# Which filter taps run on VectorE, and where the rest of them is added up

## The chip, the cores and the metric

The kernel runs on one core of a Trainium2 chip. TensorE (PE in the profile) multiplies matrices, VectorE (DVE), ScalarE (ACT) and GpSimd (POOL) work on elements, and SyncE (SP) issues the loads. The metric is the device time of one execution in microseconds (us). Three runs of the kernel before took 558.88, 558.89 and 561.23 us; the median is 558.89.

## The reference, cut to what matters

One decoder layer on 256 positions of width 1024. The input is normed and projected; two mixers run side by side, a convolution module and a sparse attention with three branches; their gated sum, a cross-attention and a feed-forward net follow. The change touches the first mixers only:

```python
def conv_module(u, dw_w, dw_b, ln_g, ln_b, pw_w):
    a, gt = jnp.split(u, 2, axis=-1)
    v = a * jax.nn.sigmoid(gt)
    v = lax.conv_general_dilated(v, dw_w[:, None, :], window_strides=(1,),
        padding=((CONV_WIDTH - 1, 0),), feature_group_count=CONV_CH, ...) + dw_b   # 31 taps per channel
    v = jax.nn.silu(layer_norm(v, ln_g, ln_b))
    return v @ pw_w
...
p_cmp = masked_softmax(s_c, dist_c >= 0)                       # compressed branch: 15 blocks of keys
o_cmp = jnp.einsum("bgrsn,bngd->bsgrd", p_cmp, v_cmp)
...
p = masked_softmax(s, mask)                                    # selected and window branch, head by head
```

## The kernel before, in words

Channels lie on the 128 partitions and positions along the free axis, so the 1024 channels of the convolution are eight blocks of 128 channels by 256 positions (with 30 columns of padding ahead). A tap multiplies one shifted block by one weight per channel and adds it to the block's sum.

**Weights.** Each weight matrix comes in halves of 128 x 1024 numbers. `split` (L173, L175) makes two parts of a half for three reduced matmuls (`rows`, L240): ScalarE copies the high part, and the difference, the low part, is made by GpSimd for the matrices from u1 to ga1 and by VectorE for all others. A load buffer (four of them) is free again when both parts are made; the parts have five buffers each. A low part is used by TensorE in the third of its three rounds.

**Taps.** `tapped` runs the taps of two blocks in turn on VectorE: the first tap is a `tensor_scalar` (L406), each other one a `scalar_tensor_tensor` (L408) that reads the shifted block from SBUF and the running sum from PSUM; the last one writes to `yt`. All four pairs of blocks go through one generator, and `convolve(n, ...)` draws n tap instructions from it at given places in the program: 13 behind each projection u1 to u7, 14 behind kc and vc, 11 behind each q, and so on, and what is left behind vw. They get a late priority there, so the scheduler lays them into gaps of VectorE's order. The last pair (blocks 6 and 7) stops eight taps early; `late_taps` makes those eight: ScalarE multiplies (L420, one instruction for each block), GpSimd adds to `yt` (L421, one for both blocks), and this needs VectorE's part of `yt` to be complete.

**Start of the attention heads.** The gates ga and gc, the compressed scores and the scores of the heads follow on TensorE. VectorE adds the bias to the compressed scores (L664), takes the minimum and subtracts it (L804, L805); ScalarE takes the exponential (L810); VectorE sums, inverts and multiplies (L811 to L816). For each pair of heads `scores` reduces (L707, L712), ScalarE exponentiates (L722, L726), and `weights` makes the row sum (L729), its reciprocal (L731) and eight multiplications (L734, L736) on VectorE. TensorE then transposes the compressed weights (L848) and the heads' weights (L747). VectorE also makes the masked values `vcm` (L829), which TensorE needs in `output`. The layer norm of the convolution begins with `layer_norm_sum` on GpSimd (L599, L601, L293); its mean is used on TensorE in the turn of the third pair of heads.

The order on each engine is set by the tile scheduler from the program's order, priorities and the marks of `behind(...)` ("issue only after these"). Each engine works strictly through its own order.

## Time and profile before

The profiled execution took 558.54 us; its span on the core is 556.7 us.

| what | us |
|---|---|
| TensorE busy | 543.3 (98% of the span) |
| VectorE busy | 467.1 (84%) |
| ScalarE busy | 349.5 (63%) |
| GpSimd busy | 129.9 (23%) |
| mean granted clock of TensorE | 0.994 |
| VectorE busy from 100 to 180 us | 78.5 of 80 |
| GpSimd busy from 40 to 140 us | 83.3 of 100 |

A row of the timeline has start and length in us, engine, line, operation, output and inputs, shape and count; what stands in brackets is the idle time of the engine just before and what ended it. A row of the waits has who waited for whom, the total in us, how often and the longest. A row of windows has the busy time of each engine in a stretch, then TensorE's granted clock (1.00 is full), the share of the DMA engines and GB/s.

### The profile page before, as it was taken

Reading aid. Unit: us, or ns where it says so; the run is one execution under the profiler, and the core shown is the slowest. Engines: PE = TensorE matmul, PEld = TensorE weight load, DVE = VectorE, ACT = ScalarE, POOL = GpSimd, SP = SyncE. Lnnn points to the kernel's source line nnn. Section 1 sums busy time; section 2 is a strip of 40 time slices with the busy share of each in tenths; the row PEclk is TensorE's granted clock in tenths of the full one; section 3 lists DMA queues with packets and bytes.
Section 4 is the critical chain, followed back from the end, with each engine's and each line's share of the span. In section 5 each row is a group of like instructions: output and inputs, shape, how many; then the busy total and the mean of one; then the engine's idle time right before and its main releaser. Section 6 shows DMA issues by size and latency. Waiting matters only on the chain.

```text
span 556.7 us, 10484 instructions
## 1 busy us (share of the span) xinstructions
PE 543.3 (98%) x3976; PEld 502.8 (90%) x3976; DVE 467.1 (84%) x940; ACT 349.5 (63%) x622; POOL 129.9 (23%) x86
## 2 busy tenths in 40 slices
PE   9999999999997899999999999999999999999995
PEld 7999999999997798998999999988888888888774
DVE  3987898999999988795768676577899998869996
ACT  4763466666464887779646655466666676655563
POOL 0089798788009200300003100150000000000000
PEclk9999999999999999999999999999999999999998
DMA  8938936465251654335555733545645654525541
GB/s 303 399 113 276 351 107 225 159 203 186 77 167 42 194 167 132 97 113 173 180 191 172 270 119 100 172 144 162 216 152 194 203 198 162 176 89 190 195 146 75
DMA packets 29155, 97.32 MB, mean 175 GB/s; under 512 B 3120, under 2 KB 5680, under 8 KB 28848
## 3 DMA queue, kind: packets, MB, share of 16 engines
q1 hardware_dynamic: 28384, 95.42, 51.4%
q10 hardware_dynamic: 720, 1.23, 0.6%
q8 instruction: 31, 0.51, 0.4%
q14 instruction: 20, 0.16, 0.1%
HBM read 95.39 MB, written 1.25 MB: 174 GB/s over the span
## 4 chain that ended last, share of the span: by engine, by line
PE 82%; DVE 11%; DMA 3%; ACT 2%; issue 1%; ACTq 0%; DVEq 0%; SPq 0%
PE ps_f L1131 15%; PE ps_u L240 8%; PE ps_f L1133 7%; PE ps_pw L240 4%; PE ps_q L240 4%; PE ps_xq L240 4%; PE ps_v L240 4%; PE ps_wo L240 4%; PE ps_xo L240 4%; PE ps_k L240 3%; PE ps_ga L240 3%; PE ps_gc L240 2%; DMA fo<-in_wfo_dram 2%; DVE fo_1l L175 2%; DVE tr L1074 2%
## 5 line engine op out<-in xcount | busy, mean ns | idle before, releaser
L408 DVE SCALAR_TENSOR_TENSOR yp<-vt,ppt,yp 128x256 f32<-128x256 f32 x216 | 86.8, 481 | 0.3
L1131 PE MATMUL ps_f<-g,f_1h 128*128 128x512 f32 x176 | 48.9, 397 | 0.0
L1131 PE MATMUL ps_f<-g,f_0h 128*128 128x512 f32 x176 | 48.3, 396 | 0.0
L1131 PEld LDWEIGHTS ps_f<-g,f_1h 128*128 128x128 f32 x176 | 32.8, 188 | 7.5
L1131 PEld LDWEIGHTS ps_f<-g,f_0h 128*128 128x128 f32 x176 | 30.1, 188 | 4.0
L175 DVE TENSOR_TENSOR f_1l<-f,f_1h 128x1024 fp32r<-128x1024 f32 x22 | 27.5, 1248 | 5.5 <-ACT f_1h L173 4.0
L1133 PEld LDWEIGHTS ps_f<-g,f_0l 128*128 128x128 f32 x176 | 27.0, 189 | 3.9
L175 DVE TENSOR_TENSOR f_0l<-f,f_0h 128x1024 fp32r<-128x1024 f32 x22 | 26.8, 1218 | 1.7 <-ACT f_0h L173 1.7
L1133 PE MATMUL ps_f<-g,f_0l 128*128 128x256 f32 x176 | 28.2, 282 | 0.0
L173 ACT ACTIVATE f_1h<-f 128x1024 fp32r<-128x1024 f32 x22 | 23.2, 1057 | 7.4 <-PE ps_xo L240 3.7
L1133 PE MATMUL ps_f<-g,f_1l 128*128 128x256 f32 x176 | 26.5, 281 | 0.0
L175 POOL TENSOR_TENSOR u_0l<-u,u_0h 128x1024 fp32r<-128x1024 f32 x7 | 17.4, 2491 | 31.4 <-DVE kt L486 29.8
L173 ACT ACTIVATE f_0h<-f 128x1024 fp32r<-128x1024 f32 x22 | 23.1, 1050 | 1.4 <-PE ps_xo L240 1.3
L1134 ACT ACTIVATE ab<-ps_f 128x256 f32<-128x256 f32 x44 | 16.6, 377 | 10.9 <-PE ps_f L1133 10.2
L1133 PEld LDWEIGHTS ps_f<-g,f_1l 128*128 128x128 f32 x176 | 23.3, 188 | 0.0
L1135 DVE TENSOR_TENSOR ab<-ps_f,ab 128x256 f32<-128x256 f32 x44 | 18.4, 419 | 5.3 <-ACT ab L1134 5.0
L722 ACT ACTIVATE p<-p,mins 128x256 f32<-128x256 f32 x32 | 15.9, 499 | 10.3 <-DVE mins L707 10.3
L284 ACT ACTIVATE uh<-sl 128x256 fp32r<-128x256 f32 x22 | 9.1, 414 | 14.6 <-DVE sl L1139 14.6
L421 POOL TENSOR_TENSOR yt<-yt,vw 128x512 f32<-128x512 f32 x8 | 11.6, 1455 | 28.3 <-DVE yt L408 27.8
L175 POOL TENSOR_TENSOR u_1l<-u,u_1h 128x1024 fp32r<-128x1024 f32 x7 | 18.0, 2578 | 0.0
L1138 ACT ACTIVATE sl<-ab 128x256 f32<-128x256 f32 x22 | 9.2, 417 | 13.5 <-DVE ab L1136 13.5
L173 ACT ACTIVATE fo_1h<-fo 128x1024 fp32r<-128x1024 f32 x10 | 10.6, 1057 | 8.8 <-DMA fo<-in_wfo_dram 7.1
(613 smaller groups left out, 1669.9 us busy)
## 6 DMA issues: line engine op xcount, KB each, us to landing
f<-in_wst_dram SPq DMA_DIRECT2D x44, 512.0 KB, 6.0
fo<-in_wfo_dram SPq DMA_DIRECT2D x22, 512.0 KB, 4.2
u<-in_wst_dram SPq DMA_DIRECT2D x14, 512.0 KB, 7.6
q<-in_wst_dram SPq DMA_DIRECT2D x8, 512.0 KB, 5.2
ga<-in_wst_dram SPq DMA_DIRECT2D x8, 512.0 KB, 3.4
gc<-in_wst_dram SPq DMA_DIRECT2D x8, 512.0 KB, 3.8
v<-in_wst_dram SPq DMA_DIRECT2D x8, 512.0 KB, 5.7
pw<-in_wst_dram SPq DMA_DIRECT2D x8, 512.0 KB, 4.6
```

Of the source, the lines that this page charges most:

```text
L173: copy = nc.scalar.activation(hi, w, AF.Copy)
L175: splits[name] = copy, eng.tensor_tensor(out=lo, in0=w, in1=f(hi[:]), op=ALU.subtract)
L240: mm = nc.tensor.matmul(ps[:, b], lhsT=lhsT, rhs=rhs, start=row + b + kb == 0, stop=kb == NB - 1 and row == 2 and b == 1)
L408: nc.vector.scalar_tensor_tensor(out=yt[:, k] if t == ts[-1] else acc[i], in0=v, scalar=w, in1=acc[i], op0=ALU.mult, op1=ALU.add)
L421: nc.gpsimd.tensor_tensor(out=yt[:, j:j + 2], in0=yt[:, j:j + 2], in1=pr, op=ALU.add)
L722: exp.append(nc.scalar.activation(p1[k][:, br], p1[k][:, br], AF.Exp, scale=-1.0, bias=mins[:, hd, 1, br:br + 1], accum_out=sums[:, hd, 1, ...
L1074: return nc.vector.tensor_tensor(out=tr[:, to], in0=pick(a), in1=pick(b), op=ALU.subtract)
L1131: nc.tensor.matmul(ps, lhsT=hs[kb // 4][0][:, kb % 4, cs], rhs=fg[:, :, kb], start=kb == 0, stop=False)
L1133: nc.tensor.matmul(ps[:, 1], lhsT=hs[kb // 4][1][:, kb % 4, cs], rhs=fg[:, 0, kb], start=False, stop=kb == NB - 1)
L1134: nc.scalar.activation(ab[:, b], ps[:, 0], AF.Copy)
L1135: nc.vector.tensor_tensor(out=ab[:, b], in0=ps[:, 1], in1=ab[:, b], op=ALU.add)
L1138: silu = nc.scalar.activation(sl, ab[:, 0], AF.Silu)
```

## The change

Of the first pair of blocks, taps 0 to 17 go to ScalarE and GpSimd, and taps 18 to 30 stay on VectorE and end in a separate tile `part01`. ScalarE writes tap 0 with the bias straight into `yt`, each other tap into a buffer (four of them, tag "vw"); GpSimd adds the seventeen buffers and at last `part01`. The other three pairs have all 31 taps on VectorE, and `late_taps` is gone. `convolve` takes two numbers now: how many tap instructions of VectorE to draw (as before) and how many taps of the other generator. The masked values are made by GpSimd behind the low part of the second half of ga0, and `layer_norm_sum` stands behind the last multiplication of the compressed softmax.

```diff
-LATE = 8
+FIRST_G = 18
...
-    def tapped(j, ts):
+    def taps_v(j, ts, out):
         acc = [aux(f"yp{j + i}", [P, S], "pt", 2) for i in range(2)]
...
-                if t == 0:
-                    nc.vector.tensor_scalar(out=acc[i], in0=v, scalar1=w, scalar2=col(PP_DB, k), op0=ALU.mult, op1=ALU.add)
+                if t == ts[0]:
+                    nc.vector.tensor_scalar(out=acc[i], in0=v, scalar1=w, scalar2=col(PP_DB, k) if t == 0 else 0.0,
+                                            op0=ALU.mult, op1=ALU.add)
...
-    taps = chain(*[tapped(j, range(TAPS - LATE * (j == 6))) for j in range(0, NB, 2)])
-
-    def late_taps(j, *marks):
-
-        with behind(*marks):
-            for t in range(TAPS - LATE, TAPS):
-                pr = small(f"vw{j}_{t}", [P, 2, S], tag="vw", bufs=4)
-                for i in range(2):
-                    nc.scalar.activation(pr[:, i], vt[j + i][:, t:t + S], AF.Copy, scale=col(PP_DW + TAPS * (j + i), t))
-                nc.gpsimd.tensor_tensor(out=yt[:, j:j + 2], in0=yt[:, j:j + 2], in1=pr, op=ALU.add)
+    def taps_g(ts):
+
+        for t in ts:
+            pr = yt[:, 0:2] if t == 0 else small(f"vw{t}", [P, 2, S], tag="vw", bufs=4)
+            for i in range(2):
+                nc.scalar.activation(pr[:, i], vt[i][:, t:t + S], AF.Identity, scale=col(PP_DW + TAPS * i, t),
+                                     bias=col(PP_DB, i) if t == 0 else 0.0)
+            if t > 0:
+                nc.gpsimd.tensor_tensor(out=yt[:, 0:2], in0=yt[:, 0:2], in1=pr, op=ALU.add)
+            yield
+        nc.gpsimd.tensor_tensor(out=yt[:, 0:2], in0=yt[:, 0:2], in1=part01, op=ALU.add)
+        yield
+
+    part01 = small("part01", [P, 2, S], tag="pr", bufs=4)
+    taps = range(TAPS)
+    on_v = chain(taps_v(0, taps[FIRST_G:], part01), *[taps_v(j, taps, yt[:, j:j + 2]) for j in range(2, NB, 2)])
+    on_g = taps_g(taps[:FIRST_G])
...
-        convolve(13 * (j > 0), act, vec)
+        convolve(13 * (j > 0), (0, 1, 1, 1, 1, 0, 1, 1)[j], act, vec)
...
-        convolve(13 + NB * TAPS * br, act, splits[name + "_1"][0])
+        convolve(13 + NB * TAPS * br, 1 + TAPS * br, act, splits[name + "_1"][0])
...
+    hm = cpt[:, CP_HM:CP_HM + 8].unsqueeze(2).to_broadcast([P, 8, HD])
+    with behind(splits["ga0_1"][1]):
+        for i in range(2):
+            nc.gpsimd.tensor_tensor(out=vcm[:, 8 * i:8 * i + 8], in0=vcs[:, i].unsqueeze(1).to_broadcast([P, 8, HD]), in1=hm, op=ALU.mult)
...
-    late_taps(6, splits["ga1_1"][1])
...
-    total = layer_norm_sum()
+    with behind(vec):
+        total = layer_norm_sum()
...
-                with behind(*first["scores"]):
-                    hm = cpt[:, CP_HM:CP_HM + 8].unsqueeze(2).to_broadcast([P, 8, HD])
-                    for i in range(2):
-                        nc.vector.tensor_tensor(out=vcm[:, 8 * i:8 * i + 8], in0=vcs[:, i].unsqueeze(1).to_broadcast([P, 8, HD]),
-                                                in1=hm, op=ALU.mult)
```

In the changed file the lines move: a tap on VectorE is L409, one on ScalarE L418, an add L421, the add of `part01` L423, the mask L660, the norm's sum L608 and L610; the heads' weights are L742 (sum), L744 (reciprocal), L747 and L749 (multiplications), their score reductions L720 and L725, the exponentials L735 and L739, the compressed softmax L817, L818, L823 and L824 to L829, its transposes L857. TensorE's order is the same in both. Three places of the other engines' orders follow (names end in a running number of the tile).

GpSimd from the last weight splits (`ga_0l`, `ga_1l`) to the sum of the norm, before and then now:

```order
L175 TENSOR_TENSOR ga_0l<-ga_0_1924,ga_0h 128x1024
L175 TENSOR_TENSOR ga_1l<-ga_1_1967,ga_1h 128x1024
L421 TENSOR_TENSOR yt<-yt,vw_23_2013 128x512
L421 TENSOR_TENSOR yt<-yt,vw_24_2017 128x512
...
L421 TENSOR_TENSOR yt<-yt,vw_28_2033 128x512
L599 TENSOR_TENSOR ysum<-yt 128x512
L421 TENSOR_TENSOR yt<-yt,vw_29_2037 128x512
L421 TENSOR_TENSOR yt<-yt,vw_30_2041 128x512
L601 TENSOR_TENSOR ysum<-ysum,yt 128x512 x2
```

```order
L175 TENSOR_TENSOR ga_0l<-ga_0_1978,ga_0h 128x1024
L421 TENSOR_TENSOR yt<-yt,vw_1763 128x512
L660 TENSOR_TENSOR vals<-vcs,cpt 128x512 x2
L175 TENSOR_TENSOR ga_1l<-ga_1_2021,ga_1h 128x1024
L421 TENSOR_TENSOR yt<-yt,vw_1867 128x512
...
L421 TENSOR_TENSOR yt<-yt,vw_1887 128x512
L423 TENSOR_TENSOR yt<-yt,part_362 128x512
L608 TENSOR_TENSOR ysum<-yt 128x512
L610 TENSOR_TENSOR ysum<-ysum,yt 128x512 x2
```

Eleven of the seventeen adds now stand between earlier splits (the last of these is the second row here), and six behind the last split; before, all eight stood there.

VectorE at the compressed scores (`nsc`), before and then now:

```order
L664 TENSOR_TENSOR nsc<-cs_ps_1995,nsc 128x256
L175 TENSOR_TENSOR ga_1l<-ga_1_2217,ga_1h 128x1024
L175 TENSOR_TENSOR gc_0l<-gc_0_2277,gc_0h 128x1024
L175 TENSOR_TENSOR gc_1l<-gc_1_2307,gc_1h 128x1024
L408 SCALAR_TENSOR_TENSOR yp_1718<-vt_354,ppt,yp_1718 128x256
L408 SCALAR_TENSOR_TENSOR yt<-vt_354,ppt,yp_1717 128x256
L804 TENSOR_REDUCE mc<-nsc 128x32
L408 SCALAR_TENSOR_TENSOR yt<-vt_354,ppt,yp_1718 128x256
L805 TENSOR_TENSOR nsc<-nsc,mc 128x512
L729 SCALAR_TENSOR_TENSOR sums<-sums,igd 128x8
```

```order
L678 TENSOR_TENSOR nsc<-cs_ps_2049,nsc 128x256 x2
L175 TENSOR_TENSOR ga_1l<-ga_1_2239,ga_1h 128x1024
L175 TENSOR_TENSOR gc_0l<-gc_0_2297,gc_0h 128x1024
L817 TENSOR_REDUCE mc<-nsc 128x32
L175 TENSOR_TENSOR gc_1l<-gc_1_2327,gc_1h 128x1024
L818 TENSOR_TENSOR nsc<-nsc,mc 128x512
L742 SCALAR_TENSOR_TENSOR sums<-sums,igd 128x8
```

The last taps (`yp`, `yt`) are gone from this place; they stand ahead of the first `nsc` add now.

VectorE between the scores of the second and third pair of heads (`p_4` and `p_5` are third-pair score tiles, `p_2` and `p_3` second-pair ones), before and then now:

```order
L829 TENSOR_TENSOR vals<-vcs,cpt 128x512 x2
L175 TENSOR_TENSOR gc_0l<-gc_0_2384,gc_0h 128x1024
...
L769 SCALAR_TENSOR_TENSOR sga<-sga,o_2398 128x256
L707 ISA p_4_2419,mins<-s_4_2414,nb_2409 128x256
...
L712 ISA p_2_2413,mins<-s_2_2412,nb_2409 128x128
L712 ISA mins 128x1
L729 SCALAR_TENSOR_TENSOR sums<-sums,igd 128x8
L175 TENSOR_TENSOR gc_0l<-gc_0_2676,gc_0h 128x1024
L731 RECIPROCAL sums<-sums 128x8
L734 TENSOR_SCALAR p_2_2259<-p_2_2259,sums 128x256
```

```order
L782 SCALAR_TENSOR_TENSOR sga<-sga,o_2418 128x256
L720 ISA p_4_2439,mins<-s_4_2434,nb_2429 128x256
L720 ISA mins 128x1
L742 SCALAR_TENSOR_TENSOR sums<-sums,igd 128x8
L720 ISA p_4_2439,mins<-s_4_2434,nb_2429 128x256
L720 ISA mins 128x1
L744 RECIPROCAL sums<-sums 128x8
L720 ISA p_5_2447,mins<-s_5_2442,nb_2429 128x256
...
L747 TENSOR_SCALAR p_2_2281<-p_2_2281,sums 128x256
```

The mask (`vals`) and one weight split no longer stand ahead of the second pair's multiplications, and the row sum and reciprocal stand inside the third pair's reductions.

More of the change, by code (lines that the diff above doesn't have):

```diff
@@ L404, in tapped, with convolve @@
                 v, w = vt[k][:, t:t + S], col(PP_DW + TAPS * k, t)
-                if t == 0:
-                    nc.vector.tensor_scalar(out=acc[i], in0=v, scalar1=w, scalar2=col(PP_DB, k), op0=ALU.mult, op1=ALU.add)
+                if t == ts[0]:
+                    nc.vector.tensor_scalar(out=acc[i], in0=v, scalar1=w, scalar2=col(PP_DB, k) if t == 0 else 0.0,
+                                            op0=ALU.mult, op1=ALU.add)
                 else:
-                    nc.vector.scalar_tensor_tensor(out=yt[:, k] if t == ts[-1] else acc[i], in0=v, scalar=w, in1=acc[i],
+                    nc.vector.scalar_tensor_tensor(out=out[:, i] if t == ts[-1] else acc[i], in0=v, scalar=w, in1=acc[i],
                                                    op0=ALU.mult, op1=ALU.add)
                 yield
-    taps = chain(*[tapped(j, range(TAPS - LATE * (j == 6))) for j in range(0, NB, 2)])
-    def late_taps(j, *marks):
-        with behind(*marks):
-            for t in range(TAPS - LATE, TAPS):
-                pr = small(f"vw{j}_{t}", [P, 2, S], tag="vw", bufs=4)
-                for i in range(2):
-                    nc.scalar.activation(pr[:, i], vt[j + i][:, t:t + S], AF.Copy, scale=col(PP_DW + TAPS * (j + i), t))
-                nc.gpsimd.tensor_tensor(out=yt[:, j:j + 2], in0=yt[:, j:j + 2], in1=pr, op=ALU.add)
-    def convolve(n, *marks):
+    def taps_g(ts):
[13 more added lines that the diff above has]
+    on_g = taps_g(taps[:FIRST_G])
+    def convolve(n_v, n_g, *marks):
         here = tc.cur_priority
@@ L427, in convolve @@
         with behind(*marks):
-            for _ in range(n):
-                next(taps, None)
+            for work, n in ((on_v, n_v), (on_g, n_g)):
+                for _ in range(n):
+                    next(work, None)
         tc.cur_priority = here
@@ L488, in tile_hybrid_block @@
                                     ppt[:, PP_POS + 16 * kv:PP_POS + 16 * kv + 16].rearrange("p (m l) -> p l m", m=2))
-        convolve(14, act, vec)
+        convolve(14, 1 - kv, act, vec)
     kcp = small("kcp", [P, GROUPS, 2, 16], F32R)
@@ L544, in tile_hybrid_block @@
                                              op0=ALU.mult, op1=ALU.subtract)
-        convolve(11, act, vec)
+        convolve(11, (1, 0, 1, 1)[j], act, vec)
         if j == 1:
@@ L559, in keys @@
                                           in1=f(kdh[lo:lo + 64, g::2, br]), op=ALU.subtract)
-        convolve(11, act, vec)
+        convolve(11, 1 - br, act, vec)
     keys(0, gemm("ks", h))
```

## The prediction

> **What bounds the kernel now.** I read the page's busy shares first, then the waits of TensorE (PE), then the order of time around the two waits that are large, and from there the engines that ended them.
>
> ```profile
> PE 543.3 (98%) x3976; PEld 502.8 (90%) x3976; DVE 467.1 (84%) x940; ACT 349.5 (63%) x622; POOL 129.9 (23%) x86
> PE pc_ps L848 <- DVE nsc L816: 3.7, 1, 3.7
> PE pt_a L747 <- DVE p L736: 1.6, 1, 1.6
> ```
>
> PE is busy for 98% of the span, so the change can only win where PE waits or runs slow. Both large waits lie in the stage that starts the attention heads, and VectorE (DVE) ends both. TensorE there, start and length in us, with the same transposes in an undisturbed place (215 us) below; the last row is the window behind the first wait (busy us of PE, weight load, DVE, ACT and POOL, then granted clock, DMA share and GB/s):
>
> ```profile
> 173.91 1.10 PE L240 MATMUL ps_gc<-hl,gc_1h 128*128 128x256 f32 x8
> 178.69 1.11 PE L848 MATMUL pc_ps<-cpt,nsc 128*128 128x128 f32 x4 [3.67 <-DVE nsc L816]
> 179.59 1.92 PE L747 MATMUL pt_a<-cpt,p 128*128 128x128 f32 x8
> 181.91 1.19 PE L240 MATMUL ps_gc<-hh,gc_1l 128*128 128x256 f32 x8
> ...
> 190.21 1.10 PE L240 MATMUL ps_gc<-hl,gc_1h 128*128 128x256 f32 x8
> 192.96 1.81 PE L747 MATMUL pt_a<-cpt,p 128*128 128x128 f32 x8 [1.65 <-DVE p L736]
> 194.97 1.20 PE L240 MATMUL ps_gc<-hh,gc_1l 128*128 128x256 f32 x8
> ...
> 214.15 1.11 PE L240 MATMUL ps_gc<-hl,gc_1h 128*128 128x256 f32 x8
> 215.09 1.03 PE L747 MATMUL pt_a<-cpt,p 128*128 128x128 f32 x8
> 215.96 0.60 PE L747 MATMUL pt_b<-cpt,p 128*128 128x128 f32 x4
> 216.32 1.19 PE L240 MATMUL ps_gc<-hh,gc_1l 128*128 128x256 f32 x8
> 178.70:183.00 4.30, 4.30 (x25) 4.30 (x26) 4.30 (x18) 1.58 (x3) 4.06 (x4) 0.64 0.08 25
> ```
>
> The first wait costs more than 3.67 us: in the stretch behind it (last row) the granted clock is 0.64. At the second, the eight transposes take 2.01 us until the next gate matmul instead of 1.23, because they follow the weights one by one as DVE delivers them. Start to start: 173.91 to 181.91 is 8.00 us. Undisturbed it is 0.94 (214.15 to 215.09) + 0.43 (four transposes, half of the 0.87 from 215.09 to 215.96) + 1.23 = 2.60; lost 5.40. 190.21 to 194.97 is 4.76, undisturbed 0.94 + 1.23 = 2.17; lost 2.59. Together **7.99 us** of PE time hang on DVE here.
>
> Why DVE is late, from its own order of time, and what GpSimd (POOL) and ScalarE (ACT) do then:
>
> ```profile
> 166.31 0.68 DVE L805 TENSOR_TENSOR nsc<-nsc,mc 128x512 f32<-128x512 f32 x1
> 166.91 1.28 DVE L729 SCALAR_TENSOR_TENSOR sums<-sums,igd 128x8 f32<-128x8 f32 x1
> 169.62 1.38 DVE L736 TENSOR_SCALAR p<-p,sums 128x128 f32<-128x128 f32 x1
> 175.42 0.67 DVE L811 TENSOR_REDUCE sumc<-nsc 128x32 f32<-128x512 f32 x1
> 177.94 0.69 DVE L816 TENSOR_TENSOR nsc<-nsc,sumc 128x512 f32<-128x512 f32 x1
> 192.35 0.35 DVE L734 TENSOR_SCALAR p<-p,sums 128x256 f32<-128x256 f32 x1
> 192.62 0.28 DVE L736 TENSOR_SCALAR p<-p,sums 128x128 f32<-128x128 f32 x1
> 194.19 1.22 DVE L175 TENSOR_TENSOR gc_1l<-gc,gc_1h 128x1024 fp32r<-128x1024 f32 x1
> 166.47 8.95 POOL L421 TENSOR_TENSOR yt<-yt,vw 128x512 f32<-128x512 f32 x6 [27.80 <-DVE yt L408]
> ```
>
> The same ten weight instructions take 8.51 us for the first heads (166.91 to 175.42), and about 2.1 for the second (the eight multiplications from 192.35 to 194.19, and two small ones). The slow ones stand exactly beside GpSimd's six late adds: L736 takes 1.38 instead of 0.28. So the late taps, put on GpSimd to relieve DVE, themselves cost it some 6.4 us on the chain that PE waits for.
>
> [...]
>
> **The change part by part.** Sums go against the profiled execution, 558.54 us (span 556.7); the median of the three runs, 558.89, is 0.35 above it.
>
> *Taps leave DVE.* DVE had 31 x 8 - 16 = 232 tap instructions, now 13 x 2 + 31 x 6 = 212: 20 fewer.
>
> ```profile
> 140.48 10.67 DVE L408 SCALAR_TENSOR_TENSOR yp<-vt,ppt,yp 128x256 f32<-128x256 f32 x27
> 160.80 0.41 DVE L664 TENSOR_TENSOR nsc<-cs_ps,nsc 128x256 f32<-128x256 f32 x1
> 161.14 1.21 DVE L175 TENSOR_TENSOR ga_1l<-ga,ga_1h 128x1024 fp32r<-128x1024 f32 x1
> ```
>
> One tap costs 10.67/27 = 0.40 us, so 7.9 us leave DVE. Before, the 27 of this row and eleven later ones were left at 140.48; now 18 are, so the last ends near 140.48 + 18 x 0.40 = 147.6, and none is left in the softmax stretch. The stretch 160.80 to 166.31 loses three taps (1.2 us) and its start, four taps earlier, moves up to 0.8. L805 then comes near 164.3.
>
> *The adds leave the softmax.* Ten weight instructions at 2.1 instead of 8.5 us end near 167. But ScalarE now has the exponential of the compressed scores behind one more weight copy, which waits for a load:
>
> ```profile
> 166.30 1.07 ACT L173 ACTIVATE gc_1h<-gc 128x1024 fp32r<-128x1024 f32 x1 [2.40 <-DMA gc<-in_wst_dram]
> 169.62 0.61 ACT L810 ACTIVATE nsc<-nsc 128x512 f32<-128x512 f32 x1
> ```
>
> That load follows the release by the split at 161.14, which comes 0.8 us earlier: the copy starts near 165.5, the exponential ends near 167.2, and the five instructions L811 to L816 (175.42 to 178.63, 3.2 us) end near **170.4**. PE is there at 174.86. The 5.40 us go, with 4.4 us to spare. The clock loss goes with the idle time.
>
> *Second heads.* The mask (L829, two instructions) leaves DVE, and the row sum and reciprocal move ahead between the score reductions. From PE's end of the first heads' transposes:
>
> ```profile
> 187.24 0.39 ACT L726 ACTIVATE p<-p,mins 128x128 f32<-128x128 f32 x1
> 185.86 0.50 PE L702 MATMUL s<-kdh,qt 128*128 128x512 f32 x1
> ```
>
> The exponentials end 5.8 us after 181.91, PE's next scores begin 3.95 after it, and PE needs the weights 9.25 after it (190.21 + 0.95). With the sum at 5.9 and the rest of the scores' reductions in between (about 1.8), the eight multiplications (1.84) end 9.0 to 9.5 after it. PE takes the first ones first. I take the 2.59 us as gone; the other bound is that nothing of them goes.
>
> *What GpSimd and ScalarE take on.* Eleven adds move among the weight splits, then two mask instructions, then six adds and one for the part sum.
>
> ```profile
> L421 POOL TENSOR_TENSOR yt<-yt,vw x8: 1263/1417/1823, 166.5 to 177.9; 128x512 f32<-128x512 f32 x8
> 50.74:138.67 87.93, 87.93 (x788) 87.32 (x786) 83.69 (x201) 52.44 (x76) 72.52 (x31) 1.00 0.64 215
> 62.03 2.44 POOL L175 TENSOR_TENSOR u_0l<-u,u_0h 128x1024 fp32r<-128x1024 f32 x1 [0.34 <-ACT u_0h L173]
> 72.63 1.11 PE L240 MATMUL ps_u<-hh,u_0l 128*128 128x256 f32 x8
> 136.23 2.44 POOL L175 TENSOR_TENSOR ga_1l<-ga,ga_1h 128x1024 fp32r<-128x1024 f32 x1 [0.90 <-ACT ga_1h L173]
> 153.19 1.19 PE L240 MATMUL ps_ga<-hh,ga_1l 128*128 128x256 f32 x8
> 72.63 1.71 ACT L420 ACTIVATE vw<-vt,ppt 128x256 f32<-128x256 f32 x4 [1.25 <-DVE vt L436]
> ```
>
> From 50.74 to 138.67 GpSimd is idle for 15.4 us. Eleven adds at 1.42 and two masks (not seen on GpSimd; same size, 1.26 to 1.82, taken at 1.42) want 18.5. So the last split ends 3 to 6 us later, near 143, and PE needs it at 153.19. The tightest place is the split at 62.03, behind three adds: up to 4.3 of its 8.2 us of lead go, 3.9 remain. Cost on PE: zero. If the cover went, each us beyond would be one on PE. The seven adds behind the last split end near 154, 12 us ahead of the softmax weights. ScalarE gets 20 more taps (1.71/4 = 0.43 each, 8.6 us over 100 us of which 40% are idle), and loses eight at 170 us. The norm's sum, now behind the softmax (L816), takes 4.9 us from 170.4 and is over before the second heads' weights; PE needs it only at 204 us.
>
> Sum: 558.54 - 7.99 = 550.55; on the scale of the median, **550.9 us**.
>
> **Rivals.**
> *Contention moves along.* If GpSimd's last adds slip past 166 us, the weights again take up to 6.4 us more: L816 near 176.8, PE waits 2 us and its clock perhaps holds (at the 1.65 us wait no clock was lost); and the norm's sum, pushed to 177 to 182, meets the second heads' weights, so that the 2.59 stay. 550.9 + 2 + 2.6 = 555.5. Needs 12 us of slip; against it stands the count above. 12%.
> *The second stall stays.* The reordering brings nothing, the wait on L736 returns in part or whole: 552.5 to 553.5. For it: its margin is only +0.3 to -0.3 us. 18%.
> *The next limit takes it.* PE comes 8 us earlier to heads whose weights and biases come by DMA, and something there may not follow:
>
> ```profile
> 199.00:262.00 63.00, 63.00 (x529) 56.90 (x527) 49.41 (x169) 50.57 (x134) 4.72 (x16) 1.00 0.40 128
> ```
>
> The loads follow releases by DVE that also come earlier, and from 199 us on PE has no wait with DVE 78% busy (49.41 of 63). Half the gain would give 554.5. 9%.
> *Slower: GpSimd becomes the bound.* 29 splits lie between 50.74 and PE's need of the last at 153.19, 102.45 us, beside adds and masks of at most 13 x 1.82 = 23.7. At 2.44 a split that is 94.5. Above 2.72 us a split PE waits, above 3.0 the gain is gone, and each 0.1 us is 2.9 us on PE. One split took 3.42 us:
>
> ```profile
> 33.03 3.42 POOL L175 TENSOR_TENSOR u_1l<-u,u_1h 128x1024 fp32r<-128x1024 f32 x1
> ```
>
> If all did, 29 x 3.42 + 23.7 = 122.9: 20 us later than needed, 571 in the end. Against it: the 31 splits from 50.74 to 138.67 took 72.52 us, 2.34 each, beside the same taps of DVE. 5%.
>
> **How the numbers follow.** Forecast as summed: 56%, its own range 549.5 to 552. Below 0.5% (2.8 us) this kernel's runs tell nothing, so faster means under 556.1: the forecast, the second stall, the half gain and most of the contention case give 0.89; same 0.06; slower 0.05. The range runs from 549.4 (the sum and a run's spread of 0.3%) to 555.5, the contention case.
>
> **What would show it.** Right: no wait of PE above 0.3 us between 150 and 262 us, granted clock 1.00 from 174 to 183 (now 0.97 and 0.64), all L749 at about 0.28 us, last tap on DVE near 148, GpSimd's part add near 154, span near 549. Wrong: a PE wait on a GpSimd split before 150 us, an L749 above 1 us, or a new PE wait behind 199 us.

## The result and the profile after

The changed kernel takes 550.99 us (median of four runs, 550.18 to 551.05), the kernel before beside it 559.04 (558.88 to 561.23). The ratio is 0.9844, with a 95% interval of 0.9818 to 0.987: 8 us, or 1.6%, faster. The profiled execution has a span of 549.2 us (556.7 before). Of all runs of the kernels built from it below, one was in a slower state (560.30 us, against 550.17 to 551.20 of the same kernel) and is not read.

The page's row of busy shares, and then all that the view of waits has for TensorE:

```profile
PE 541.1 (99%) x3976; PEld 502.5 (92%) x3976; DVE 454.9 (83%) x918; ACT 356.6 (65%) x642; POOL 144.1 (26%) x98
```

```profile
PE warm L338 <- DVE eps_t L156: 1.0, 1, 1.0
PE m L1172 <- ACT ft_0h L173: 0.2, 1, 0.2
```

Both large waits, on the compressed softmax and on the second heads' weights, are gone. What is left was there before. TensorE in the stage that starts the heads, and the two windows there:

```profile
174.07 1.11 PE L240 MATMUL ps_gc<-hl,gc_1h 128*128 128x256 f32 x8
175.02 0.60 PE L857 MATMUL pc_ps<-cpt,nsc 128*128 128x128 f32 x4
175.46 1.03 PE L760 MATMUL pt_a<-cpt,p 128*128 128x128 f32 x8
...
176.68 1.18 PE L240 MATMUL ps_gc<-hh,gc_1l 128*128 128x256 f32 x8
...
184.96 1.11 PE L240 MATMUL ps_gc<-hl,gc_1h 128*128 128x256 f32 x8
185.90 1.03 PE L760 MATMUL pt_a<-cpt,p 128*128 128x128 f32 x8
...
187.13 1.19 PE L240 MATMUL ps_gc<-hh,gc_1l 128*128 128x256 f32 x8
```

```profile
174.00:178.70 4.70, 4.70 (x44) 4.70 (x43) 3.40 (x3) 2.98 (x9) 0.00 (x0) 1.00 0.79 201
178.70:183.00 4.30, 4.30 (x35) 3.27 (x35) 2.04 (x12) 4.30 (x17) 0.00 (x0) 1.00 0.92 314
```

Start to start, the two stretches that took 8.00 and 4.76 us take 2.61 (174.07 to 176.68) and 2.17 (184.96 to 187.13): 7.98 us less, and the granted clock behind is 1.00 (0.64 before). VectorE (a selection of its rows) and GpSimd around it, with ScalarE's copy ahead of the exponential of the compressed scores:

```profile
139.48 4.24 DVE L175 TENSOR_TENSOR ga_0l<-ga,ga_0h 128x1024 fp32r<-128x1024 f32 x1
149.91 0.86 DVE L409 SCALAR_TENSOR_TENSOR yt<-vt,ppt,yp 128x256 f32<-128x256 f32 x2
154.09 2.30 DVE L175 TENSOR_TENSOR ga_0l<-ga,ga_0h 128x1024 fp32r<-128x1024 f32 x1
164.61 0.69 DVE L818 TENSOR_TENSOR nsc<-nsc,mc 128x512 f32<-128x512 f32 x1
165.21 0.16 DVE L742 SCALAR_TENSOR_TENSOR sums<-sums,igd 128x8 f32<-128x8 f32 x1
167.29 0.28 DVE L749 TENSOR_SCALAR p<-p,sums 128x128 f32<-128x128 f32 x1
168.38 0.69 DVE L824 TENSOR_REDUCE sumc<-nsc 128x32 f32<-128x512 f32 x1 [0.81 <-ACT nsc L823]
169.94 0.69 DVE L829 TENSOR_TENSOR nsc<-nsc,sumc 128x512 f32<-128x512 f32 x1
180.74 0.42 DVE L782 SCALAR_TENSOR_TENSOR sga<-sga,o 128x256 f32<-128x256 f32 x1 [3.34 <-PE o L778]
```

```profile
136.96 2.07 POOL L660 TENSOR_TENSOR vals<-vcs,cpt 128x512 f32<-128x512 f32 x2
138.96 2.41 POOL L175 TENSOR_TENSOR ga_1l<-ga,ga_1h 128x1024 fp32r<-128x1024 f32 x1
141.33 9.03 POOL L421 TENSOR_TENSOR yt<-yt,vw 128x512 f32<-128x512 f32 x6
150.44 1.28 POOL L423 TENSOR_TENSOR yt<-yt,part 128x512 f32<-128x512 f32 x1
151.80 1.28 POOL L608 TENSOR_TENSOR ysum<-yt 128x512 f32<-128x512 f32 x1
153.16 4.38 POOL L610 TENSOR_TENSOR ysum<-ysum,yt 128x512 f32<-128x512 f32 x2
```

```profile
166.77 1.06 ACT L173 ACTIVATE gc_1h<-gc 128x1024 fp32r<-128x1024 f32 x1 [2.70 <-DMA gc<-in_wst_dram]
```

The ten weight instructions take 2.4 us (165.21 to 167.57) with GpSimd idle, against 8.6 (166.91 to 175.49) before. The compressed softmax is ready at 170.63, TensorE is there at 175.02. GpSimd is through with everything, the norm's sum included, at 158.4 us.

### The profile page after: what moved, and what is told of

Its sections match the earlier page's. It is cut to its first block, busy times and chain, and to the rows that moved or that the text cites. A ratio compares the mean times of both kernels' runs of the same rounds, so it can differ in the third digit from the quotient of the medians.

```text
span 549.2 us, 10508 instructions
## 1 busy us (share of the span) xinstructions
PE 541.1 (99%) x3976; PEld 502.5 (92%) x3976; DVE 454.9 (83%) x918; ACT 356.6 (65%) x642; POOL 144.1 (26%) x98
## 3 DMA queue, kind: packets, MB, share of 16 engines
HBM read 95.39 MB, written 1.25 MB: 176 GB/s over the span
## 4 chain that ended last, share of the span: by engine, by line
PE 89%; DVE 6%; DMA 2%; ACT 1%; issue 1%; DVEq 0%; SPq 0%; ACTq 0%
PE ps_f L1140 15%; PE ps_u L240 8%; PE ps_f L1142 8%; PE ps_ga L240 4%; PE ps_pw L240 4%; PE ps_q L240 4%; PE ps_xq L240 4%; PE ps_wo L240 4%; PE ps_xo L240 4%; PE ps_v L240 4%; PE ps_gc L240 4%; PE ps_k L240 3%; DMA fo<-in_wfo_dram 2%; DVE fo_1l L175 2%; PE s L715 2%; DVE tr L1083 2%
## 5 line engine op out<-in xcount | busy, mean ns | idle before, releaser
L409 DVE SCALAR_TENSOR_TENSOR yp<-vt,ppt,yp 128x256 f32<-128x256 f32 x196 | 78.5, 485 | 0.3
L1143 ACT ACTIVATE ab<-ps_f 128x256 f32<-128x256 f32 x44 | 16.5, 376 | 10.9 <-PE ps_f L1142 10.2
L421 POOL TENSOR_TENSOR yt<-yt,vw 128x512 f32<-128x512 f32 x17 | 23.0, 1353 | 0.6 <-ACT vw L418 0.2
L735 ACT ACTIVATE p<-p,mins 128x256 f32<-128x256 f32 x32 | 15.9, 503 | 11.0 <-DVE mins L720 11.0
```

The source lines that it names most:

```text
L409: nc.vector.scalar_tensor_tensor(out=out[:, i] if t == ts[-1] else acc[i], in0=v, scalar=w, in1=acc[i], op0=ALU.mult, op1=ALU.add)
L421: nc.gpsimd.tensor_tensor(out=yt[:, 0:2], in0=yt[:, 0:2], in1=pr, op=ALU.add)
L735: exp.append(nc.scalar.activation(p1[k][:, br], p1[k][:, br], AF.Exp, scale=-1.0, bias=mins[:, hd, 1, br:br + 1], accum_out=sums[:, hd, 1, ...
L1143: nc.scalar.activation(ab[:, b], ps[:, 0], AF.Copy)
```

## The experiments

**Theory:** the whole gain comes from GpSimd's additions leaving the places where VectorE makes what TensorE waits for. **Rivals:** VectorE is faster because it has 20 taps fewer; the mask had to leave it for the second wait to go; GpSimd's additions did not matter, VectorE was late for other reasons. In what follows "softmax ready" is the end of the last multiplication of the compressed softmax, and "weights" the time from the first heads' row sum to the last of the ten instructions.

### One part of the change at a time

**As few taps on GpSimd as before, but early.** One number of the changed kernel:

```diff
-FIRST_G = 18
+FIRST_G = 8
```

> The changed kernel with 8 instead of 18 taps of the first two blocks on ScalarE and GpSimd: VectorE has 31 x 8 - 16 = 232 taps, as before the change, and GpSimd adds seven buffers and the part sum early, long before the softmax. So VectorE gets no relief, and the adds still leave the softmax stretch. Theory (the adds beside the weights cost the time): VectorE's last taps come about 8 us later than in the changed kernel, up to 3.3 us of it run into the stretch behind 160 us; the ten weight instructions take 2.1 to 4 us (two adds of the norm's sum may stand beside them), the last multiplication of the compressed softmax ends 171 to 174 against TensorE's arrival at 175: no wait of TensorE, 551 to 552 us. Rival (the relief of VectorE by 20 taps is what helps): that multiplication ends at 177 or later, a wait of 2 to 4 us returns with a lowered clock, 555 to 558.5 us.

Measured 552.08 us, ratio to before 0.987 (0.986 to 0.989), just above the 551 to 552 expected. VectorE has its 232 taps back, yet 7 of the 8 us stay gained. The weights take 4.9 us, because two additions of the norm's sum stand beside them; the softmax is ready at 174.0, in time. 1.1 us are lost in another place. ScalarE's copy of the next weight there and TensorE's only new wait:

```profile
183.60 1.06 ACT L173 ACTIVATE gc_0h<-gc 128x1024 fp32r<-128x1024 f32 x1 [2.03 <-DMA gc<-in_wst_dram]
191.57 0.44 PE L775 MATMUL o<-ptt_b,vals 128*64 128x128 f32 x4 [0.90 <-ACT ptt_b L763]
```

The same copy in the changed kernel, which does not wait for its load:

```profile
181.62 1.06 ACT L173 ACTIVATE gc_0h<-gc 128x1024 fp32r<-128x1024 f32 x1
```

So there is a second deadline to keep: the four weight splits of VectorE behind the softmax (to 177.4 us in the changed kernel, to 180.7 here) give the load buffers free. In the changed kernel the load for the copy above was issued at 174.23 us, right behind the first of these splits (end 173.99); here that split ends 3.3 us later, at 177.32. So late splits make late loads, these hold up ScalarE's queue, and its copies of the transposes come late.

**The same with the order of the norm's sum changed**, so that VectorE's last pair is added last and one addition less stands beside the weights:

```diff
-        for j in (6, 4):
+        for j in (4, 6):
             nc.gpsimd.tensor_tensor(out=ysum, in0=ysum, in1=yt[:, j:j + 2], op=ALU.add)
```

> The kernel with eight taps of the first two blocks on ScalarE and GpSimd, and the norm's sum takes the pair of blocks that VectorE ends last in its last instead of its second addition. So one addition and the fold stand beside the weights, not two. Theory A (the 1.1 us that this kernel is slower than the changed one come from the two additions that hold the weights): the weights take 3.4 instead of 4.8 us, the splits end 1.3 us sooner, the wait of 0.9 us at 191 us goes to 0 to 0.3: 551.0 to 551.6 us. Theory B (from the 20 taps that VectorE keeps): 552.1 us as before.

Measured 551.14 us: theory A. The weights take 3.8 us, the softmax is ready at 173.3, and TensorE has no wait there. With the same 232 taps as before the change, this kernel stands 0.15 us from the changed one, within the spread of either. **Once the additions are gone from beside the weights, the relief of VectorE by 20 taps is worth nothing that can be measured.**

**The mask back on VectorE, no mark on the norm's sum**, taps as changed:

```diff
-    with behind(splits["ga0_1"][1]):
-        for i in range(2):
-            nc.gpsimd.tensor_tensor(out=vcm[:, 8 * i:8 * i + 8], in0=vcs[:, i].unsqueeze(1).to_broadcast([P, 8, HD]), in1=hm, op=ALU.mult)
...
-    with behind(vec):
-        total = layer_norm_sum()
+    total = layer_norm_sum()
...
+                with behind(*first["scores"]):
...
+                    for i in range(2):
+                        nc.vector.tensor_tensor(out=vcm[:, 8 * i:8 * i + 8], in0=vcs[:, i].unsqueeze(1).to_broadcast([P, 8, HD]),
+                                                in1=hm, op=ALU.mult)
```

> The changed kernel with the two mask instructions back on VectorE at their old place, behind the scores of the second pair of heads, and with the norm's sum not marked to come behind the compressed softmax; the taps stay as changed. Theory (the adds alone are the cause; mask and mark are minor): the two instructions take 2.5 to 2.8 us of VectorE's 3.3 idle us at 177 to 181, the second pair's weights come at most 0.5 us later: 551 to 551.6 us, no TensorE wait above 0.5 us. Rival (the mask must leave VectorE for the second wait to go): the wait of TensorE on the second pair's weights returns with 1.2 to 1.7 us and its transposes follow one by one, 552.5 to 553.6 us.

Measured 550.78 us (550.31 to 551.10), as the changed kernel. The two instructions take 1.28 us, half of what was expected, and lie in VectorE's idle time ahead of 180.4. The mask need not have moved, and the mark does nothing that the time shows.

**The mask alone**, in the kernel before:

```diff
+    with behind(splits["ga0_1"][1]):
+        for i in range(2):
+            nc.gpsimd.tensor_tensor(out=vcm[:, 8 * i:8 * i + 8], in0=vcs[:, i].unsqueeze(1).to_broadcast([P, 8, HD]), in1=hm, op=ALU.mult)
...
-                with behind(*first["scores"]):
...
-                    for i in range(2):
-                        nc.vector.tensor_tensor(out=vcm[:, 8 * i:8 * i + 8], in0=vcs[:, i].unsqueeze(1).to_broadcast([P, 8, HD]),
-                                                in1=hm, op=ALU.mult)
```

> The kernel before with only the two mask instructions moved to GpSimd, behind the low part of the second half of ga0; taps and late adds as before. Theory (the adds beside the weights cost the time): the first wait of 3.7 us and the low clock behind it stay, because the adds still stand beside the weights; the second wait shrinks by 0.5 to 1.65 us: 556 to 558.5 us, in the middle 557.3. Rival (the mask carries the whole second loss): 2.6 us gained, 556.2 us. Rival (the first wait comes from VectorE's load of work in general): a first wait shorter by the 2.5 us of the mask, 553.5 to 555 us.

Measured 558.26 us, ratio 0.998 (0.997 to 1.000). The second heads' stretch loses 0.56 us instead of 2.59, but half of that is paid back at the first wait. GpSimd, VectorE and TensorE there:

```profile
176.55 2.59 POOL L421 TENSOR_TENSOR yt<-yt,vw 128x512 f32<-128x512 f32 x2
177.89 1.80 DVE L821 TENSOR_TENSOR nsc<-nsc,sumc 128x512 f32<-128x512 f32 x1
179.75 1.12 PE L848 MATMUL pc_ps<-cpt,nsc 128*128 128x128 f32 x4 [4.77 <-DVE nsc L821]
```

The last multiplication of the softmax starts as before (177.89 against 177.94) but takes 1.80 instead of 0.69 us: one of GpSimd's two last additions happens to be under way when it comes. 1.1 us hang on that alone.

### GpSimd's instructions beside the weights

**Six additions put back**, in the changed kernel, behind the norm's sum and a small addition that waits for the minimum of the compressed scores; nothing uses the results:

```diff
     with behind(vec):
         total = layer_norm_sum()
+    dum = small("dum", [P, 2, S], tag="dum", bufs=1)
+    nc.gpsimd.tensor_tensor(out=dum[:, 0, 0:32], in0=mc.rearrange("p q h -> p (q h)"), in1=ysum[:, 0, 0:32], op=ALU.add)
+    nc.gpsimd.tensor_tensor(out=dum, in0=yt[:, 0:2], in1=yt[:, 2:4], op=ALU.add)
+    for _ in range(5):
+        nc.gpsimd.tensor_tensor(out=dum, in0=dum, in1=yt[:, 4:6], op=ALU.add)
```

> The changed kernel with a small addition on GpSimd that waits for the minimum of the compressed scores (VectorE, 163.5 us), and six additions of 128 x 512 behind it, all after the norm's sum is over; their results are used by nothing. So exactly six additions stand beside the weights, as before the change. Theory: from 164 to 173 us they stretch the ten weight instructions to about 8.5 us (165.2 to 173.7), the last multiplication of the compressed softmax ends near 176.9, TensorE waits 1.9 us: 552 to 554 us if its clock holds, 554.5 to 556.5 if it falls as with the nine additions (wait 3.5 us, 556.8 us). Rival (the nine additions cost 5.8 us for some other reason than their number, the same again with six): 556.8 us.

Measured 553.14 us (552.92 to 553.66), 2.15 more than without them and as expected. VectorE and TensorE:

```profile
165.28 1.25 DVE L742 SCALAR_TENSOR_TENSOR sums<-sums,igd 128x8 f32<-128x8 f32 x1
169.27 0.34 DVE L747 TENSOR_SCALAR p<-p,sums 128x256 f32<-128x256 f32 x1
169.53 1.33 DVE L749 TENSOR_SCALAR p<-p,sums 128x128 f32<-128x128 f32 x1
176.08 0.66 PE L862 MATMUL pc_ps<-cpt,nsc 128*128 128x128 f32 x4 [0.90 <-DVE nsc L829]
178.40 0.63 PE L760 MATMUL pt_b<-cpt,p 128*128 128x128 f32 x4 [0.78 <-DVE mins L725]
```

The weights take 8.6 us again, with the same pattern as before the change: the row sum 1.25, and of two multiplications one short and one of 1.3 us. The softmax is ready at 176.0 and not at 176.9 as expected, since its own five instructions run beside an idle GpSimd. The lateness is paid twice: 0.90 us at the softmax, and 0.78 at the last transposes, whose PSUM bank the second heads' reductions give free, and these stand behind the softmax on VectorE.

**Additions mixed with the norm's sum.** The same additions placed ahead of the norm's sum in the program; the scheduler mixed the two, so that nine additions and the fold stand beside the weights:

```diff
     vec = nc.vector.tensor_tensor(out=nsc, in0=nsc, in1=mc.unsqueeze(3).to_broadcast([P, 2, HEADS, 16]), op=ALU.subtract)
+    dum = small("dum", [P, 2, S], tag="vw", bufs=4)
+    with behind(vec):
+        nc.gpsimd.tensor_tensor(out=dum[:, 0, 0:32], in0=mc.rearrange("p q h -> p (q h)"), in1=mc.rearrange("p q h -> p (q h)"), op=ALU.add)
+        nc.gpsimd.tensor_tensor(out=dum, in0=yt[:, 0:2], in1=yt[:, 2:4], op=ALU.add)
+        for _ in range(5):
+            nc.gpsimd.tensor_tensor(out=dum, in0=dum, in1=yt[:, 4:6], op=ALU.add)
```

> The changed kernel with six additions of 128 x 512 put on GpSimd at the place of the six late adds of before: behind the minimum of the compressed scores on VectorE (164 us), with results that nothing uses. Nothing else moves. Theory (GpSimd's adds stretch the weight instructions beside them): the ten weight instructions that took 2.3 us (165.2 to 167.5) take 6 to 8.5, the last multiplication of the compressed softmax ends near 175.5 to 177, TensorE waits 0.5 to 2.5 us there: 551.5 to 554 us, and single multiplications of 128 x 128 show 1.3 us instead of 0.28. Rival (the stretched instructions had another cause, such as what VectorE itself had queued): the weights stay at 2.3 us and the time at 551 us.

Measured 556.80 us (555.50 to 558.74): more than expected. The weights take 11.0 us, not 6 to 8.5. TensorE's rows, and the windows behind the wait:

```profile
178.51 0.66 PE L863 MATMUL pc_ps<-cpt,nsc 128*128 128x128 f32 x4 [3.53 <-DVE nsc L835]
181.56 2.05 PE L240 MATMUL ps_gc<-hh,gc_1l 128*128 128x256 f32 x8
```

```profile
178.70:183.00 4.30, 3.52 (x23) 3.31 (x23) 4.30 (x19) 2.57 (x7) 0.00 (x0) 0.64 0.12 34
183.00:192.00 9.00, 9.00 (x60) 7.63 (x60) 6.03 (x25) 7.15 (x26) 0.00 (x0) 0.79 0.82 246
```

In this execution, the slowest of the ten (558.74 us), the clock behind the wait of 3.53 us is 0.64 and, in the next window, 0.79; eight gate matmuls take 2.05 us instead of 1.2. The step that failed in the expectation was the number of additions beside the weights, and with it the clock.

**Two additions only**, otherwise as with the six:

```diff
-    for _ in range(5):
-        nc.gpsimd.tensor_tensor(out=dum, in0=dum, in1=yt[:, 4:6], op=ALU.add)
+    nc.gpsimd.tensor_tensor(out=dum, in0=dum, in1=yt[:, 4:6], op=ALU.add)
```

> The changed kernel with only two additions beside the weights (and the small one that waits for the minimum), so that VectorE stands there as late as in the kernel with eight taps on ScalarE and GpSimd (552.1 us), but with 20 taps fewer before. The weights take 4.5 to 5 instead of 2.3 us, the compressed softmax is ready at 173, the four splits behind it end near 179.5 instead of 177.4. Theory A (552.1 us there came from the splits being late, whatever made them late): half of the 0.9 us wait at 191 us returns, 551.0 to 551.6 us. Theory B (it came from VectorE's 20 taps elsewhere): 550.8 to 551.1 us and no wait.

Measured 550.90 us: the weights take 4.3 us, the softmax is ready at 171.9, the splits end at 178.7, and nothing is lost. By time alone that is theory B; but the splits end here 2 us sooner than the 180.7 of the kernel with eight taps, and that kernel without one addition (551.14 us, splits to 180.1) had already answered for theory A. What is lost begins with splits that end somewhere between 180.1 and 180.7.

**Fills in place of the additions**:

```diff
-    nc.gpsimd.tensor_tensor(out=dum, in0=yt[:, 0:2], in1=yt[:, 2:4], op=ALU.add)
-    for _ in range(5):
-        nc.gpsimd.tensor_tensor(out=dum, in0=dum, in1=yt[:, 4:6], op=ALU.add)
+    for n in range(12):
+        nc.gpsimd.memset(dum, 0.0)
```

> The same, with twelve fills of 128 x 512 (a constant written, nothing read) in place of the six additions. [...] The time follows from the weights: each us beyond 4.5 us of stretch is one us of waiting on TensorE, so 551 to 553 us.

Measured 550.41 us. GpSimd and VectorE:

```profile
164.62 7.25 POOL L835 MEMSET dum<- 128x512 f32 x12
165.04 0.15 DVE L742 SCALAR_TENSOR_TENSOR sums<-sums,igd 128x8 f32<-128x8 f32 x1
165.80 0.62 DVE L749 TENSOR_SCALAR p<-p,sums 128x128 f32<-128x128 f32 x1
169.57 0.69 DVE L829 TENSOR_TENSOR nsc<-nsc,sumc 128x512 f32<-128x512 f32 x1
```

A fill takes 0.60 us (7.25 / 12). The row sum, with two inputs in SBUF, stays at 0.15 us beside fills and takes 1.25 beside additions; the multiplications, with one tensor in SBUF as input and output, grow from 0.28 to 0.62 beside fills and 1.33 beside additions. So in these two runs the additions, which read SBUF, stretched both, and the fills, which only write it, stretched the multiplications alone. The last multiplication of the softmax, with two inputs again, also keeps its 0.69 us at 169.57, with fills running to 171.9. The weights grew by 1.0 us only, so the time stayed under the 551 to 553 expected.

**Six additions and the mask together**: the kernel with the mask on VectorE, plus the five lines of the kernel with six additions.

> The changed kernel with the two mask instructions back on VectorE behind the scores of the second pair of heads, and with six additions on GpSimd beside the first weights (results unused): both differences at once, which singly gave 550.8 and 553.1 us. The question is whether the mask costs nothing only because VectorE idles 3.3 us there, which the six additions take away. Theory (the mask has cover only while the first softmax is on time): VectorE has no idle time left at 178 to 184 us, its two instructions (1.3 us) delay the splits and the second pair's weights by as much; TensorE meets weights that come 0.3 to 1.3 us late, or a copy of ScalarE that is as late at 193 us: 553.7 to 554.8 us. Rival (the mask is hidden in any case): 553.0 to 553.4 us. Rival (the full second wait returns): 555 us and more.

Measured 553.24 us (552.69 to 553.60), as without the mask (553.14): the first rival, not the theory. Beside this run the kernel before varied from 558.15 to 571.99 us, but the traces say the same: from the last gate matmuls ahead of the softmax to the first ones behind the second heads TensorE takes 15.3 us (173.84 to 189.15), 15.2 without the mask, 13.1 in the changed kernel. VectorE has no idle time left there, the splits end at 183.9, yet no wait on the second heads' weights comes back.

### VectorE late without GpSimd

Additions of VectorE's own, results unused, between the subtraction of the minimum and the weights; first seven, then thirteen:

```diff
+    with behind(vec):
+        for _ in range(7):
+            held_up = nc.vector.tensor_tensor(out=dum, in0=yt[:, 2:4], in1=yt[:, 4:6], op=ALU.add)
...
+        with behind(*[held_up] * (hp == 0)):
             nc.vector.scalar_tensor_tensor(out=sc, in0=sc, scalar=1e-30, in1=igd[:, 2 * hp:2 * hp + 2].rearrange("p h t b -> p (h t b)"),
...
+    with behind(held_up):
         nc.vector.tensor_reduce(out=sumc, in_=nsc, axis=AX.X, op=ALU.add)
```

> The changed kernel with seven additions of 128 x 512 on VectorE itself (0.60 us each, 4.2 us, results unused) between the subtraction of the minimum and the first weights. Nothing on GpSimd. Theory (TensorE is there 4.5 us after the compressed softmax is ready, and 0.8 us of VectorE's waiting for the exponential goes first): ready near 174.0 instead of 170.6 us, TensorE there at 175.0: no wait, 551.0 to 551.6 us. Rival (VectorE's work counts in the end whether TensorE waits there or not): 553 to 555 us.

Measured 552.39 us (551.87 to 553.06). An addition took 0.72 us, so 5.0 in all; the softmax is ready at 174.1 as expected, and TensorE does not wait for it. But the time is 1.4 above the changed kernel and out of the expected range: the splits end at 180.9, and the wait of the kernel with eight taps is there again, ended by ScalarE's copy (the row below). In this stage TensorE loses 1.0 us to the changed kernel (17.5 us from 173.97 to the row below, 16.5 there). The profiled execution, the slowest of the four, has another wait of 1.1 us on a weight copy of the feed-forward net at 513 us, which the changed kernel has with 0.2 and two kernels with additions with 0.7 and 0.9; no run here explains it.

```profile
191.51 0.44 PE L776 MATMUL o<-ptt_b,vals 128*64 128x128 f32 x4 [0.68 <-ACT ptt_b L764]
```

> The same with thirteen additions on VectorE (7.8 us). Theory: the compressed softmax is ready near 177.6 us, TensorE waits 2.6 us: 553.6 to 554.2 us with the clock at 1.00, and up to 555.5 us if it falls behind so short a wait. Rival (the wait alone counts for nothing, what cost the time before was GpSimd's use of the memory): no more than 552 us.

Measured 556.32 us (554.79 to 558.20). The softmax is ready at 178.5, and TensorE shows before's picture with GpSimd idle (the row of the wait, and the window behind it):

```profile
178.59 0.81 PE L863 MATMUL pc_ps<-cpt,nsc 128*128 128x128 f32 x4 [3.46 <-DVE nsc L835]
```

```profile
178.70:183.00 4.30, 4.30 (x24) 4.13 (x25) 4.30 (x19) 2.71 (x6) 0.00 (x0) 0.60 0.10 32
```

The kernel takes 5.3 us more than the changed one (556.32 - 550.99). In this stage it is 5.0: 7.61 us from 174.03 to 181.64, where the changed kernel takes 2.61. That is the wait of 3.46 us and the clock of 0.60 behind it, which costs some 4.30 x 0.40 = 1.7. The wait was expected at 2.6 with 0.60 us an addition; that was the size that failed. With nine additions on GpSimd and the softmax ready at the same 178.5 the time was 556.80. GpSimd's additions, then, show no harm of their own here: they make VectorE late, and lateness has this price from wherever it comes.

### More taps on GpSimd

```diff
-FIRST_G = 18
+FIRST_G = 28
...
-        convolve(13 * (j > 0), (0, 1, 1, 1, 1, 0, 1, 1)[j], act, vec)
+        convolve((0, 6, 0, 13, 13, 13, 13, 13)[j], (0, 1, 1, 1, 1, 0, 1, 1)[j], act, vec)
```

> The changed kernel with 28 instead of 18 taps of the first two blocks on ScalarE and GpSimd; VectorE has 192 taps, 20 fewer again (it draws fewer at two early places, since the second pair of blocks is not there sooner). Sixteen additions and that of the part sum stand behind the last weight split: 17 x 1.3 us from 141.4 reach 163.5 us, the norm's sum about 168 us or later, so three or four of these stand beside the weights again. Theory: VectorE's further relief brings nothing, as TensorE has no wait there to give back, and the last additions cost up to what the six cost (553.1 us): 551 to 553.5 us. Rival (VectorE's relief goes on paying): under 550 us.

Measured 557.22 us, ratio 0.997 (0.995 to 0.998): worse than expected, nearly all of the gain lost. The view of TensorE's waits, and ten of GpSimd's additions:

```profile
PE s L717 <- ACT sgt L695: 1.6, 1, 1.6
PE pc_ps L857 <- DVE nsc L829: 1.6, 1, 1.6
PE o L775 <- ACT ptt_b L763: 1.1, 1, 1.1
PE pt_b L760 <- DVE mins L725: 0.8, 1, 0.8
```

```profile
150.69 17.02 POOL L421 TENSOR_TENSOR yt<-yt,vw 128x512 f32<-128x512 f32 x10 [0.30 <-ACT vw L418]
```

GpSimd's additions reach 167.7 us and the norm's sum 175.3, so that splits, subtraction and weights of VectorE from 162 to 175 us are all stretched (a split takes up to 2.31 us instead of 1.22, the subtraction 1.77 instead of 0.69, the weights 5.9 instead of 2.4); and ScalarE, with 20 taps more, makes `sgt` (the exponentials of the heads' gates) 1.6 us late (first row), which the expectation did not have. The four waits are 5.1 of the 6.2 us lost. VectorE has the fewest taps of all kernels here, and its softmax is ready as late as before the change.

### All kernels in one table

Sorted by time; "ready" is the softmax's end, the waits are TensorE's there and on the second heads' weights.

| kernel | taps on VectorE | weights us | ready | waits us | clock behind | median us |
|---|---|---|---|---|---|---|
| twelve fills | 212 | 3.4 | 170.3 | 0 / 0 | 1.00 | 550.41 |
| mask back | 212 | 2.4 | 170.1 | 0 / 0 | 1.00 | 550.78 |
| two additions | 212 | 4.3 | 171.9 | 0 / 0 | 1.00 | 550.90 |
| changed | 212 | 2.4 | 170.6 | 0 / 0 | 1.00 | 550.99 |
| eight taps, last pair last | 232 | 3.8 | 173.3 | 0 / 0 | 1.00 | 551.14 |
| eight taps | 232 | 4.9 | 174.0 | 0 / 0 | 1.00 | 552.08 |
| seven on VectorE | 212 | 2.8 | 174.1 | 0 / 0 | 1.00 | 552.39 |
| six additions | 212 | 8.6 | 176.0 | 0.90 / 0 | 1.00 | 553.14 |
| six additions and mask | 212 | 8.5 | 176.0 | 1.07 / 0 | 1.00 | 553.24 |
| thirteen on VectorE | 212 | 2.8 | 178.5 | 3.46 / 0 | 0.60 | 556.32 |
| nine additions | 212 | 11.0 | 178.5 | 3.53 / 0 | 0.64 | 556.80 |
| 28 taps | 192 | 5.9 | 178.5 | 1.55 / 0 | 1.00 | 557.22 |
| mask alone | 232 | 8.6 | 179.7 | 4.77 / 0 | 0.60 | 558.26 |
| before | 232 | 8.6 | 178.6 | 3.67 / 1.65 | 0.64 | 559.04 |

The time goes broadly with "ready" and not with the taps on VectorE. (With 28 taps TensorE itself comes 1.6 us later, so its wait is shorter; in the kernel before, the second wait comes on top.) The kernels were measured in groups. The kernel before, run beside four of them, had medians of 559.04 to 559.21 us, so a few tenths between kernels of two groups say nothing.

## Why the prediction was right, and where its steps were not

**The two waits and their price: right.** 8.00 and 4.76 us became 2.61 and 2.17, as the undisturbed place at 215 us had it (2.60 and 2.17); 7.98 us against 7.99. The sum came out at 550.9 against 551.0 measured. That it is within 0.1 us is partly luck: the prediction reckoned against the profiled execution, and from profile to profile the change saved 7.56 us (558.54 to 550.98), not 7.99.

**The adds leave the softmax: right, and shown to be the cause.** Six additions put back bring back weights of 8.6 us (six additions); the adds gone with VectorE's 232 taps kept is worth the whole gain (eight taps, last pair last). L818 came at 164.61 (predicted 164.3), L829 ended at 170.6 (170.4).

Two steps to that 170.4 were off and cancelled. The exponential was to end near 167.2, because the weight copy ahead of it would come 0.8 us earlier. The load was issued 0.5 us earlier (161.89 against 162.41) but the copy started later, at 166.77 (166.30 before), and the exponential ended at 168.35. The five instructions behind it were counted at 3.2 us, as measured beside GpSimd's additions, though the same paragraph takes these away: alone they took 2.25 (168.38 to 170.63).

Six additions put back cost 2.2 us, not 8. VectorE starts the weights 1.6 us sooner than before (165.28 against 166.91) and the five softmax instructions run 1.0 us shorter, so the softmax is ready at 176.0 and not at 178.6. With additions beside the weights the earlier start, which the fewer taps give, does count; without them it falls into time that VectorE has to spare.

**Taps leave DVE: the count was right, the effect nil and one term missed.** The last tap ran to 150.8, not 147.6. The taps took 0.40 us each (16 in 6.36) beside GpSimd, but a split of VectorE, 1.22 us before, took 4.24 (139.48) beside a split and an addition of GpSimd. The prediction's sums have no term for a split of VectorE beside the moved adds. It cost nothing, because VectorE then waits for the compressed scores.

**Second heads: right number, causes only in part as told.** The prediction credited the 2.59 us to the mask leaving and to the new order. The eight multiplications ended 8.8 us behind 176.68 (9.0 to 9.5 predicted), 0.4 ahead of TensorE. But with the mask back on VectorE the 2.59 us stay gone, even with the weights stretched (six additions and mask), so its leaving was not needed. VectorE in the kernel before, and the mask's row with it back on VectorE in the changed kernel:

```profile
180.77 2.59 DVE L829 TENSOR_TENSOR vals<-vcs,cpt 128x512 f32<-128x512 f32 x2
183.28 1.76 DVE L175 TENSOR_TENSOR gc_0l<-gc,gc_0h 128x1024 fp32r<-128x1024 f32 x1
```

```profile
172.21 1.28 DVE L837 TENSOR_TENSOR vals<-vcs,cpt 128x512 f32<-128x512 f32 x2
```

Before, GpSimd was still at its last additions and the norm's sum there (busy 4.06 of the 4.30 us to 183): mask and split took 1.8 us longer than alone (1.28 and 1.22), and the chain was already late. That is the same contention, one stage on, and the prediction's working of this part does not have it. The mask's own kernel tells lateness and order apart. VectorE there, at the first score reduction:

```profile
187.69 0.42 DVE L712 CUSTOM_DVE_ANT_0 p<-s,nb 128x256 f32<-128x256 f32 x1 [0.16 <-PE s L707]
```

It is no longer late, as it waits for TensorE's scores, and 2.03 of the 2.59 us are gone. The 0.56 us left stand with the old order, in which a weight split of 1.22 us lies between the row sum and the multiplications. All kernels made from the changed one keep the new order, so no run undoes it; and no run says how the 2.03 us of lateness divide between the mask's own time and the stretching.

**What GpSimd takes on: right in the verdict, high in the prices.** A mask instruction took 1.03 us, not 1.42, an addition 1.35 on average; the last split ended at 141.4 (predicted 143), the part sum was added by 151.7 (154). The rival by which GpSimd becomes the bound did not come: no wait of TensorE on a split. (The prediction counts 29 splits in one place and 31 in another; the trace has 30 from 50.74 us on, 2.42 us each, which changes nothing.)

**The norm's sum: wrong.** "From 170.4, behind the softmax": it ran from 151.80. So the mark of `behind` put no wait into this program, and the sum does not issue only after the softmax, as the description of the kernel has it: nothing stands ahead of it on GpSimd any more, and it starts when its operands are there. Beside it a split and the gate's `igc` at 154 to 157 us took 2.30 and 1.27 us (1.22 and 0.17 in the kernel before), some 2 us more, where VectorE has them to spare.

**"4.4 us to spare" was too generous.** That holds for the softmax alone. A softmax ready at 173.3 costs nothing, one at 174.0 (eight taps) or 174.1 (seven on VectorE) costs 1.0 us of TensorE's time in this stage, through the splits, their loads and ScalarE's copies: about 3 us to spare. The rival that the next limit takes the gain named this chain (releases by VectorE, then loads); it exists, and the change stays 3 us short of it. The rival that contention moves along came true in part with 28 taps: the weights were stretched and the clock held, as it said, but no second wait came back, and ScalarE's late `sgt` came on top.

## What to carry to other kernels

Here the work given to GpSimd to relieve VectorE was paid for by the VectorE instructions that stood beside it: by those with two inputs in SBUF (the row sum took 1.25 us beside additions, 0.16 alone) and by the multiplications from SBUF to SBUF (1.33 and 0.28), not by the taps, whose second input is in PSUM (0.40 us each beside additions and alone). What mattered was not how much was moved but beside which instructions it landed, so put it where the consumer has slack. Find the slack by following every consumer of the late engine, weight splits and load buffers among them, and not only the wait that the profile names. Before a part of a change is credited, run it alone and run the rest without it: here the whole gain stayed without the mask's move and, in another run, without VectorE's relief (no run leaves out both).
